# A hybrid encoder block on one core: meta keys of four heads transposed at once, and fillers of the matmul queue placed otherwise

## The chip, the core and the metric

The kernel runs on one core of a Trainium2 chip. A core has a matrix engine (PE, whose weight loads are listed apart as PEld), a vector engine (DVE), an activation engine (ACT), a general engine (POOL) and SP, which here only issues DMAs. Each takes its instructions in the order of its own queue, and engines wait for each other through semaphores. The metric is the device time of one execution in microseconds (us); lower is better.

## What is computed

One encoder layer on 512 tokens, 16 learned meta tokens and width 1024, all in float32. Two token mixers run side by side and are merged by sigmoid gates; an output projection and a gated feed-forward follow.

```python
u = rms_norm(h, pre_mix_gain[l])
proj = u @ w_in[l]
qa, ka, va, qb, kb, vb, g = jnp.split(proj, SPLITS, axis=-1)
...
o_swa = windowed_gqa_sink_attention(qa, ka, va, attn_sink[l], pos, is_real)
...
o_diff = differential_attention(qb, kb, vb, lam, lambda_init, diff_subln_gain[l], is_key)
gates = jax.nn.sigmoid(g + b_gate[l])
g_swa, g_diff = gates[..., :D_MODEL], gates[..., D_MODEL:]
merged = g_swa * (o_swa @ w_branch_swa[l]) + g_diff * (o_diff @ w_branch_diff[l])
h = h + rms_norm(merged @ w_out[l], post_mix_gain[l])
```

In the windowed attention (SWA), 16 query heads share 4 key heads, and a block of 128 queries sees two or three blocks of 128 keys, the 16 meta keys and a sink. The differential attention has 8 heads over all 528 keys, each with two softmaxes.

## The kernel before

Every float32 operand is split into a high part, rounded to a format that PE takes at full rate, and a low part, the rest; a product of two operands is three PE products (high-high, high-low, low-high, `mm3`, lines 286 to 288). A weight tile of 1024 x 128 therefore costs a DMA (`wr`), an ACT cast (`wh`), a subtraction on POOL or DVE (`wl`) and 8 x 3 matmuls into one of three PSUM banks `pr`.

**Start.** Keys and values of SWA are projected by hand-ordered code (to line 479). A transposed row of norms gives `rbc`; DVE multiplies the table `rot` of rotations by it (line 458) and then rotates keys and queries (`ta`, `tb`, line 528) and scales the values (`VT`, line 562), which PE transposes (lines 568 and 573).

**Both attentions** are written as tasks with estimated costs and priorities; `Plan.run` (line 175) places them by list scheduling and so sets each engine's order by hand. Weights of gates and later heads are *fillers*: PE takes three of their matmuls whenever an attention step isn't ready. Which filler may be taken where is written in a few loops (lines 929 to 967).

**SWA** works in 16 units (4 key heads x 4 query blocks). For each of four query heads of a unit PE makes the scores `Sw` (line 674), DVE adds the mask and finds the minimum (line 677), ACT takes the exponential (681), DVE the reciprocal (686), POOL scales `p` (688). Queries reach their place by 16 DMAs `Q<-hl` for each group of four heads (line 550). Then PE transposes `p` block by block, four transposes at a time into one of two banks `tr` (line 705); ACT and DVE split the result into `ah` and `al`, and PE multiplies by the values into the one bank `O` (line 717). The 16 meta keys are a block of their own: four transposes of 128 x 16, an ACT cast and a DVE subtraction of 16 x 512 into rows 0 to 15 and 32 to 47 of `aTm`, and one product with `Vm` (line 710). `O` is emptied through `otmp` and `of`.

**Differential attention** has the same steps (`Sd` line 808, `Od` lines 853 to 863). After the last head, a chain of ACT and DVE steps gives `dh`, `dl`, the split output, eight tiles along the contracted axis. The last branch product (`w_bd`, lines 981 to 987) contracts over these eight for each of eight output tiles, all eight in order for one tile before the next. Then `w_out`, the norms and the feed-forward follow.

## Time and profile before

| quantity | value |
|---|---|
| median of 3 runs | 998.64 us (998.15 to 1000.51) |
| the profiled execution's own time | 999.2 us |
| its span in the profile | 997.3 us |
| mean granted PE clock | 0.992 |

The span runs from the first to the last instruction of the program; 1.9 us of the profiled execution's time lie around it. Busy time of an engine is the time in which some instruction of it was under way. A matmul's record lasts longer than the step to the next one, since matmuls are pipelined; what a matmul costs in a stream is the step between two starts. "Idle before" an instruction, with what ended it, is the time in which its engine had nothing under way.

### The profile page before, as it was taken

The numbers are of one execution on the slowest core, as the hardware profiler recorded it, in microseconds if no ns is written. First come the engines' busy times: TensorE is split into PE (matmuls) and PEld (weight loads), VectorE is DVE, ScalarE is ACT, GpSimd is POOL, SyncE is SP. The second block draws the span as 40 slices with busy tenths as digits, with TensorE's granted clock in tenths as the row PEclk, the third lists the DMA queues.
The fourth block names the chain that finished last, engine by engine and source line by source line (L and its number), as shares of the span: only waits on it lengthen the run. The fifth ranks groups of instructions, "written<-read, shape, count | busy, mean of one in ns | idle before, by whom it ended". The sixth has DMA issues, their size and how long they took to land.

```text
span 997.3 us, 14285 instructions
## 1 busy us (share of the span) xinstructions
PE 969.2 (97%) x5355; PEld 833.7 (84%) x5355; DVE 574.1 (58%) x1015; ACT 451.8 (45%) x828; POOL 278.7 (28%) x242
## 2 busy tenths in 40 slices
PE   9899999999999999999998999999999999999997
PEld 9777887889898999989886888998888888888885
DVE  5746876888575668888774756843332423323224
ACT  6336865785545544577645333633232322312221
POOL 1344344533223332334202412463433400000000
PEclk9999999999999999999999999999999999999999
DMA  9483122141534324415431461353233232234212
GB/s 332 136 213 85 43 78 80 35 129 64 130 100 112 104 68 129 128 46 156 141 106 57 147 219 41 107 170 106 88 103 98 93 105 91 100 103 130 64 64 84
DMA packets 37140, 109.33 MB, mean 110 GB/s; under 512 B 6080, under 2 KB 6592, under 8 KB 37072
## 3 DMA queue, kind: packets, MB, share of 16 engines
q1 hardware_dynamic: 37072, 108.42, 36.1%
q8 instruction: 42, 0.69, 0.3%
q14 instruction: 26, 0.21, 0.1%
HBM read 87.04 MB, written 2.10 MB: 89 GB/s over the span
## 4 chain that ended last, share of the span: by engine, by line
PE 86%; DVE 7%; ACT 3%; issue 2%; SPq 1%; DMA 1%; DVEq 0%; ACTq 0%
PE pr L287 18%; PE pr L288 18%; PE pr L286 18%; PE Sd L808 3%; PE wk L288 2%; PE wk L286 2%; PE Sw L674 2%; PE wk L287 2%; PE tr L705 2%; PE O L717 2%; PE tr L288 2%; PE tr L287 2%; PE tr L286 2%; PE tr L848 2%; PE Od L861 1%
## 5 line engine op out<-in xcount | busy, mean ns | idle before, releaser
L252 POOL TENSOR_TENSOR wl<-wr,wh 128x768 fp32r<-128x768 f32 (+1 forms) x76 | 167.9, 2210 | 242.0 <-ACT wh L271 158.1
L286 PE MATMUL pr<-xh,wh 128*128 128x264 f32 (+1 forms) x616 | 201.2, 327 | 0.0
L288 PE MATMUL pr<-xh,wl 128*128 128x264 f32 (+1 forms) x616 | 197.4, 320 | 0.3 <-DVE wl L252 0.2
L287 PE MATMUL pr<-xl,wh 128*128 128x264 f32 (+1 forms) x616 | 197.4, 320 | 0.2
L271 ACT CAST wh<-wr 128x1024 fp32r<-128x1024 f32 x78 | 82.0, 1052 | 224.6 <-PE pr L287 88.8
L252 DVE TENSOR_TENSOR wl<-wr,wh 128x1024 fp32r<-128x1024 f32 (+2 forms) x110 | 109.8, 999 | 117.6 <-ACT wh L271 108.5
L288 PEld LDWEIGHTS pr<-xh,wl 128*128 128x128 f32 x616 | 116.8, 190 | 9.3 <-POOL wl L252 0.5
L287 PEld LDWEIGHTS pr<-xl,wh 128*128 128x128 f32 x616 | 117.1, 190 | 7.9 <-DVE xl L378 0.6
L286 PEld LDWEIGHTS pr<-xh,wh 128*128 128x128 f32 x616 | 117.1, 190 | 7.3 <-ACT wh L256 0.2
L287 PE MATMUL pr<-ul,wh 128*128 128x512 f32 (+1 forms) x304 | 110.7, 364 | 0.3 <-DVE ul L252 0.3
L286 PE MATMUL pr<-uh,wh 128*128 128x512 f32 (+1 forms) x304 | 110.9, 365 | 0.0
L288 PE MATMUL pr<-uh,wl 128*128 128x512 f32 (+1 forms) x304 | 110.6, 364 | 0.0
L503 ACT CAST wh<-wr 128x1024 fp32r<-128x1024 f32 x56 | 58.4, 1048 | 39.4 <-PE pr L287 31.3
L287 PEld LDWEIGHTS pr<-ul,wh 128*128 128x128 f32 x304 | 57.3, 189 | 9.7 <-DVE ul L252 0.5
L288 PEld LDWEIGHTS pr<-uh,wl 128*128 128x128 f32 x304 | 57.4, 189 | 9.1
L286 PEld LDWEIGHTS pr<-uh,wh 128*128 128x128 f32 x304 | 57.3, 189 | 9.0
L540 POOL TENSOR_TENSOR ta<-ta,tb 128x528 f32<-128x528 f32 (+1 forms) x26 | 36.3, 1395 | 87.9 <-DVE tb L528 77.4
L813 DVE TENSOR_REDUCE nm<-Sd 128x1 f32<-128x528 f32 x64 | 45.1, 704 | 17.5 <-PE Sd L808 16.4
L308 POOL TENSOR_TENSOR r3y<-r3v,mhalf 128x1 f32<-128x1 f32 x4 | 2.2, 549 | 186.7 <-DVE r3v L307 186.7
L688 POOL TENSOR_SCALAR p<-p,rc 128x272 f32<-128x272 f32 (+1 forms) x64 | 37.0, 591 | 61.2 <-DVE rc L686 59.6
L816 ACT ACTIVATE pp<-Sd,nm 128x528 f32<-128x528 f32 x40 | 28.0, 700 | 46.4 <-DVE nm L813 27.7
L808 PE MATMUL Sd<-Kd,Qd 128*128 128x264 f32 x256 | 43.3, 291 | 3.3 <-ACT pp L816 3.1
(366 smaller groups left out, 2003.4 us busy)
## 6 DMA issues: line engine op xcount, KB each, us to landing
wr<-in_w_in_dram SPq DMA_DIRECT2D x50, 512.0 KB, 4.0
wr<-in_w_fi_dram SPq DMA_DIRECT2D x50, 512.0 KB, 3.5
wr<-in_w_fo_dram SPq DMA_DIRECT2D x22, 512.0 KB, 3.4
Kd<-hl SPq DMA_DIRECT2D x32, 132.0 KB, 2.4
Kd<-Kd SPq DMA_DIRECT2D x16, 264.0 KB, 3.4
Q<-hl SPq DMA_DIRECT2D x64, 64.0 KB, 2.0
Qd<-hl SPq DMA_DIRECT2D x64, 64.0 KB, 2.7
wr<-in_w_bs_dram SPq DMA_DIRECT2D x8, 512.0 KB, 3.5
```

The costliest lines, as they stand in the source:

```text
L252: (eng or dve).tensor_tensor(out=lo, in0=src, in1=hi.bitcast(F32), op=ALU.subtract)
L271: act.copy(out=wh, in_=raw)
L286: pe.matmul(out=ps, lhsT=ah, rhs=bh, start=first, stop=False)
L287: pe.matmul(out=ps, lhsT=ah, rhs=bl, start=False, stop=False)
L288: pe.matmul(out=ps, lhsT=al, rhs=bh, start=False, stop=last)
L503: T("ACT", 1.05, lambda: act.copy(out=wh.t, in_=wr.t), r=[wr], w=[wh], prio=pr_)
L540: T("POOL", 0.05 + 1.3 * m, lambda: pool.tensor_tensor(out=ta.t[:, :, 0:n], in0=ta.t[:, :, 0:n], in1=tb.t[:, :, 0:n], op=ALU.add), r=[tb], ...
L674: pe.matmul(out=Sw2[:, S.slot, 0:nk], lhsT=QS[g][hh].t[:, i * P:(i + 1) * P], rhs=KB[g].t[:, x, r0:r1], start=(x == 0), stop=(x == 1))
L688: T("POOL", 0.2 + 0.43 * c, lambda z=z: pool.tensor_scalar(out=pt.t[:, z, 0:nk], in0=pt.t[:, z, 0:nk], scalar1=rc.t[:, z:z + 1], scalar2=1 ...
L808: pe.matmul(out=S.t[:, s, 0:HALF], lhsT=Q[c].t[:, i * P:(i + 1) * P], rhs=K[c].t[:, x, s * HALF:(s + 1) * HALF], start=(x == 0), stop=(x = ...
L813: T("DVE", 0.71, lambda S=S, c=c, one=one: dve.tensor_reduce(out=nm.t[:, c, one], in_=S.t[:, :, 0:HALF], axis=AX.XY, op=ALU.min), r=[S], w ...
L816: T("ACT", 0.9, lambda S=S, c=c, one=one, p=p: act.activation(out=p().rearrange("p (a b) -> p a b", a=2), in_=S.t[:, :, 0:HALF], func=AF.E ...
```

## The change

**Meta keys of SWA.** The 16 meta columns of four heads are first copied by POOL into one tile `pm` of 128 x 128 (each head's 16 twice). One PE transpose replaces four. ACT makes the high part of all 128 rows (`ma`), and four DVE instructions write, for each head, 32 rows of a block-diagonal operand (16 rows high part with its sign turned, 16 rows low part; two columns of signs are new in `vec`). The product with `Vm` is still one matmul, with `Vm` repeated for the four heads and now the last of its unit. Two such operands (`aTm`, `bdm`) take turns. The meta rows of the values are prepared likewise. `otmp` and `of`, through which `O` is emptied, become one tile `ot`.

```diff
+        def meta():
+            tm, w, pm = bank("tr", 2, "tr"), sb("ma", [P, P], F32R, "ma", 3), sb("ma", [P, 4, 2, NMETA], F32, "pm", 3)
...
+            T("POOL", 0.34, lambda: pool.tensor_copy(
+                out=pm.t, in_=pt.t[:, :, mo:mo + NMETA].unsqueeze(2).broadcast_to([P, 4, 2, NMETA])),
+                r=ph, w=[pm], keep=[pt], prio=0)
+            Ttr[u].append(T("PE", 0.14, lambda: pe.transpose(
+                out=tm.t[:, 0:P], in_=pm.t.rearrange("p a b c -> p (a b c)"), identity=ident),
+                r=[pm], w=[tm], prio=0, chain="tr"))
+            T("ACT", 0.32, lambda: act.copy(out=w.t, in_=tm.t[:, 0:P]), r=[tm], w=[w], prio=1, chain="ah")
+            for hh in range(4):
+                rs, cs = slice(32 * hh, 32 * hh + 32), slice(hh * P, (hh + 1) * P)
+                T("DVE", 0.24, lambda rs=rs, cs=cs: dve.scalar_tensor_tensor(
+                    out=bd[rs, cs], in0=tm.t[rs, 0:P], scalar=low[rs], in1=w.t[rs].bitcast(F32), op0=ALU.mult,
+                    op1=ALU.subtract), r=[tm, w], w=[D_], prio=1)
...
+            if n == 0:
+                meta()
...
+        T("PE", mm_t(512), lambda: pe.matmul(out=O.t, lhsT=VM[g // 2].t[:, g % 2].rearrange("p a b -> p (a b)"),
+                                             rhs=bd, start=False, stop=True), r=[D_, VM[g // 2]], w=[O], prio=0)
```

**The table of rotations** becomes a task with a late priority, and the first three weight loads are told to land sooner.

```diff
-    dve.tensor_tensor(out=rot, in0=rot, in1=rbc.unsqueeze(1).broadcast_to([P, 3, EXT]), op=ALU.mult)
...
+    T("DVE", 1.84, lambda: dve.tensor_tensor(out=rot, in0=rot, in1=rbc.unsqueeze(1).broadcast_to([P, 3, EXT]),
+                                             op=ALU.mult), w=[ROT], prio=5)
...
-          w=[wr], dep=dep, prio=pr_, land=3.6)
+          w=[wr], dep=dep, prio=pr_, land=3.6 if nfill[0] > 3 else 0.3)
```

DVE's order at the start, where `rb` are columns of the norms and `kraw` the raw keys; before:

```order
L454 COPY rb<-r0y 128x128
L458 TENSOR_TENSOR rot<-rot,rbc 128x1584
L528 TENSOR_TENSOR ta<-kraw,rot 128x528
L528 TENSOR_TENSOR tb<-kraw,rot 128x528
L528 TENSOR_TENSOR ta<-kraw,rot 128x528
L562 TENSOR_TENSOR VT<-tr,rbc 128x264 x2
```

and the same place in the changed kernel:

```order
L456 COPY rb<-r0y 128x128
L567 TENSOR_TENSOR VT<-tr,rbc 128x264 x2
L630 TENSOR_TENSOR rot<-rot,rbc 128x1584
L471 ISA lj,ls<-lt 128x64
L471 ISA ls 128x1
```

The values `VT` now stand ahead of `rot` and of the three rotations.

**Fillers.** Gates 2 to 5 are released behind units 0, 1, 2 and 8 instead of 2 and 3 behind units 1 and 5; two gates instead of four stay behind SWA; the branch products of SWA are spread 4, 3, 0, 1 instead of 3, 3, 2 over the differential heads.

```diff
-        for j in {1: (2,), 5: (3,)}.get(u, ()):
+        for j in {0: (2,), 1: (3,), 2: (4,), 8: (5,)}.get(u, ()):
...
-    for j in (4, 5, 6, 7):
+    for j in (6, 7):
...
-        for _ in range((3, 3, 2, 0, 0, 0, 0, 0)[h]):
+        for _ in range((4, 3, 0, 1, 0, 0, 0, 0)[h]):
```

SP's order ahead of the first scores, where `Q` are the queries of the first group, `hl` their rotated source and `wr` weights; before:

```order
L501 DMA wr<-in_w_in_dram 128x1024 x3
L550 DMA Q<-hl 32x512 x12
L501 DMA wr<-in_w_in_dram 128x1024 x2
L550 DMA Q<-hl 32x512 x4
L501 DMA wr<-in_w_in_dram 128x1024
```

and in the changed kernel:

```order
L506 DMA wr<-in_w_in_dram 128x1024 x2
L555 DMA Q<-hl 32x512 x8
L506 DMA wr<-in_w_in_dram 128x1024
L555 DMA Q<-hl 32x512 x4
L506 DMA wr<-in_w_in_dram 128x1024
L555 DMA Q<-hl 32x512 x4
L506 DMA wr<-in_w_in_dram 128x1024
```

The last four queries now stand behind one load that directly precedes them instead of two; the other load stands four queries earlier.

**The last branch product** takes the first seven of the eight contracted tiles for output tiles 0 and 1, and only then the eighth for both.

```diff
+    first = [(load_w(I["w_bd"][j]), pr_t()) for j in range(2)]
+    for b in first:
+        bd_products(b, range(KT - 1))
     for j in range(KT):
-        w = load_w(I["w_bd"][j])
-        pb = pr_t()
-        proj(pb, w, (dh, dl), 0, NTOK)
+        b = first[j] if j < 2 else (load_w(I["w_bd"][j]), pr_t())
+        bd_products(b, range(KT - 1 if j < 2 else 0, KT))
+        pb = b[1]
```

PE's order where the eighth tile of `dh` is first needed (the row that waits for ACT), before:

```order
L287 MATMUL pr_5964<-dl_4018,wh_5960 128x512
L288 MATMUL pr_5964<-dh_4017,wl_5961 128x512
L286 MATMUL pr_5964<-dh_4017,wh_5960 128x512 [waits Activation_49]
L287 MATMUL pr_5964<-dl_4018,wh_5960 128x512 [waits DVE_49]
L288 MATMUL pr_5964<-dh_4017,wl_5961 128x512
L286 MATMUL pr_6000<-dh_4017,wh_5995 128x512
```

and in the changed kernel, where `pr_6001` is output tile 0 and `pr_6009` output tile 1:

```order
L287 MATMUL pr_6009<-dl_4309,wh_6004 128x512
L288 MATMUL pr_6009<-dh_4308,wl_6005 128x512 [waits DVE_49]
L286 MATMUL pr_6001<-dh_4308,wh_5997 128x512 [waits Activation_49]
L287 MATMUL pr_6001<-dl_4309,wh_5997 128x512 [waits DVE_49]
L288 MATMUL pr_6001<-dh_4308,wl_5998 128x512
L286 MATMUL pr_6009<-dh_4308,wh_6004 128x512
```

Twenty-one products of output tile 1 now stand between the seventh and the eighth contracted tile of output tile 0.

## Prediction

> **What bounds the kernel now.** I read first the page's busy times and its chain of work, then PE's waits, longest first, then the stages.

> ```profile
> PE 969.2 (97%) x5355; PEld 833.7 (84%) x5355; DVE 574.1 (58%) x1015; ACT 451.8 (45%) x828; POOL 278.7 (28%) x242
> ...
> PE 86%; DVE 7%; ACT 3%; issue 2%; SPq 1%; DMA 1%; DVEq 0%; ACTq 0%
> ```

> PE is busy for 97% of the span and makes 86% of the chain. So a matmul less, or a PE wait less, shortens the run; time saved on another engine does so only where PE waits for it. Where it waits:

> ```profile
> PE Sw L674 <- DVE nm L677: 4.2, 9, 0.9
> PE pr L286 <- ACT dh L898: 4.1, 1, 4.1
> ...
> PE Sw L674 <- issue: 2.1, 1, 2.1
> PE tr L568 <- DVE VT L562: 1.8, 1, 1.8
> ...
> PE tr L573 <- DVE VT L562: 1.1, 1, 1.1
> ```

> Four single waits make 9.1 us: 4.1 for the last head's output, 2.1 ahead of the first scores, 1.8 and 1.1 for the values at the start. The change touches all four. By stage (span, then PE busy, PEld, DVE, ACT, POOL, granted clock):

> ```profile
> 74.90:225.00 150.10, 145.06 (x806) 120.07 (x807) 114.40 (x295) 107.22 (x260) 63.63 (x92) 0.98 0.27 75
> 225.00:536.50 311.50, 306.59 (x2015) 276.41 (x2013) 219.69 (x387) 173.45 (x323) 87.53 (x64) 1.00 0.37 104
> ...
> 545.00:985.00 440.00, 439.66 (x2091) 370.23 (x2091) 181.03 (x236) 134.17 (x185) 98.85 (x55) 1.00 0.33 104
> ```

> SWA (75 to 225) and differential attention (225 to 536) each leave PE idle for about 5 us (150.1 less 145.1; 311.5 less 306.6). From 545 on PE has no slack: what is gained ahead of it reaches the end.

> Idle PE time costs a second time, through the clock:

> ```profile
> 29.24:32.65 3.41, 1.54 (x13) 1.14 (x12) 3.41 (x10) 0.43 (x1) 1.70 (x1) 1.00 0.02 7
> 32.65:36.07 3.42, 3.42 (x18) 3.42 (x17) 3.36 (x8) 3.42 (x8) 2.68 (x2) 0.50 0.01 2
> 73.61:77.03 3.42, 1.68 (x8) 1.23 (x9) 1.07 (x4) 0.71 (x4) 1.81 (x1) 1.00 0.24 47
> 77.03:80.44 3.41, 3.41 (x12) 2.84 (x13) 0.93 (x4) 2.21 (x7) 0.00 (x0) 0.50 0.31 123
> ...
> 537.83:541.24 3.41, 0.51 (x1) 0.19 (x1) 2.73 (x4) 1.34 (x2) 1.19 (x1) 1.00 0.19 38
> 541.24:544.65 3.41, 3.25 (x8) 2.59 (x9) 2.06 (x3) 1.04 (x1) 1.30 (x1) 0.50 0.31 123
> ```

> Each time, a stretch of 3.41 us in which PE was busy for at most 1.7 us is followed by one at a clock of 0.50. In the third a product of 512 columns steps by 0.43 us (below) instead of 0.23; eight of them lose 8 x 0.20 = 1.6 us, which I take for each stretch.

> **A. Meta transposes.** Three of four go, in 16 units.

> ```profile
> 102.14 0.60 PE L705 MATMUL tr<-ident,p 128*128 128x128 f32 x4
> 104.35 0.60 PE L705 MATMUL tr<-ident,p 128*16 128x128 f32 x4
> ...
> 119.55 1.04 PE L705 MATMUL tr<-ident,p 128*128 128x128 f32 x8
> 120.34 0.48 PE L286 MATMUL pr<-xh,wh 128*128 128x512 f32 x1
> 120.66 0.39 PE L287 MATMUL pr<-xl,wh 128*128 128x512 f32 x1
> ```

> Eight transposes and a product take 120.66 - 119.55 = 1.11 us; less 0.23 for the product, 0.11 each. Four of 16 columns last as long as four of 128 (0.60), so 48 transposes are 48 x 0.11 = **5.3 us** of PE, in a stage in which PE is busy for 97%.

> In their place other engines get work:

> ```profile
> L688 POOL TENSOR_SCALAR p<-p,rc 128x400 f32<-128x400 f32 x32 | 20.9, 667 | 28.4 <-DVE rc L686 28.4
> L688 POOL TENSOR_SCALAR p<-p,rc 128x272 f32<-128x272 f32 x32 | 16.1, 516 | 32.8 <-DVE rc L686 31.2 <-PE pr L288 1.6
> L252 DVE TENSOR_TENSOR aTm<-tr,aTm 16x512 fp32r<-16x512 f32 x16 | 10.9, 680 | 3.2 <-ACT aTm L580 2.9
> L580 ACT CAST aTm<-tr 16x512 fp32r<-16x512 f32 x16 | 9.2, 574 | 5.1 <-PE tr L705 4.9
> ...
> L252 DVE TENSOR_TENSOR Vm<-tr,Vm 16x128 fp32r<-16x128 f32 x2 | 0.5, 269 | 0.0
> L580 ACT CAST Vm<-tr 16x128 fp32r<-16x128 f32 x2 | 0.5, 246 | 0.9 <-PE tr L568 0.9
> ```

> POOL: (667 - 516)/128 = 1.18 ns for an element, so the copy of 128 takes 516 - 144 x 1.18 = about 0.35 us; 16 are 5.6 us on an engine busy for 64 of 150. ACT: 0.25 for 0.57, less. DVE: four of 128 elements, 4 x 0.27 = 1.08 for 0.68, so 0.40 more in each unit, 6.4 in all. PE waits for DVE in this stage, so this costs between nothing (all beside PE's products) and 6.4 (all ahead of scores). It is not below nothing, as no DVE work goes. DVE's 114.4 us of work leave PE 4.2 us of waits, which is near the lower end: I take **2 us lost**.

> **B. The last branch product.**

> ```profile
> 526.72 2.09 POOL L252 TENSOR_TENSOR wl<-wr,wh 128x768 fp32r<-128x768 f32 x1 [20.53 <-ACT wh L271]
> ...
> 540.65 0.69 DVE L252 TENSOR_TENSOR dl<-ob,dh 128x512 fp32r<-128x512 f32 x1 [0.68 <-ACT dh L898]
> ...
> 540.67 0.51 PE L286 MATMUL pr<-dh,wh 128*128 128x512 f32 x1 [4.12 <-ACT dh L898]
> 541.40 0.80 PE L287 MATMUL pr<-dl,wh 128*128 128x512 f32 x1 [0.22 <-DVE dl L252]
> 541.99 0.63 PE L288 MATMUL pr<-dh,wl 128*128 128x512 f32 x1
> 542.42 0.63 PE L286 MATMUL pr<-dh,wh 128*128 128x512 f32 x1
> ```

> PE stops at 536.55 (540.67 less 4.12), having done seven of the eight contracted tiles of output tile 0 as it is. The change puts 7 x 3 = 21 products of output tile 1 there: 21 x 0.23 = 4.8 us, against 4.1 + 0.2 of waits. Their low weights are done at 528.8. The chain to `dh` is not touched, so PE comes to it at 541.4, when `dl` is just ready (541.3): 4.3 us of waits go, and the slow clock with them, 1.6: **5.9 us**. The cover has 0.5 us to spare; what the chain is later than that is lost.

> **C. The start.**

> ```profile
> 27.23 1.81 DVE L458 TENSOR_TENSOR rot<-rot,rbc 128x1584 f32<-128x1584 f32 x1 [0.98 <-ACT rbc L457]
> ...
> 30.93 0.77 DVE L562 TENSOR_TENSOR VT<-tr,rbc 128x264 f32<-128x264 f32 x2
> ```

> The values (0.77) now come first, at 27.2, and are ready at 28.0 instead of 31.7. PE asks for them nine products after the transposes of the norms, at about 27.5, so 0.6 remains of 1.8 + 1.1; the second half stands behind 39 products instead of 24. With the wait the clock's drop at 32.65 goes: 2.3 + 1.6 = **3.9 us**. Late instead are `rot` and the key rotations, by 0.8 us; the keys are not needed before the first scores.

> **D. The first scores.**

> ```profile
> 57.97 8.71 SPq L550 DMA_DIRECT2D Q<-hl  x12
> 66.80 2.26 SPq L501 DMA_DIRECT2D wr<-in_w_in_dram  x2
> 69.11 2.41 SPq L550 DMA_DIRECT2D Q<-hl  x4
> ...
> 74.89 0.85 PE L674 MATMUL Sw<-KK,Q 128*128 128x272 f32 x4 [2.11 <-issue]
> ...
> DMA to landing us min/median/max: 1.9/3.1/5.9
> ```

> The page names no releaser, but the last four queries, issued from 69.11 behind two weight loads, land up to 5.9 us later, at 75.0: that is the wait. The queries follow from PE's products, so they come 3.9 us earlier with C, and now behind one load: issued at 65.2, landed between 68.3 (median) and 71.1. PE comes to the scores at 72.8 - 3.9 + 1.4 (six more filler products) = 70.3. I take the wait as gone, as one load less lies ahead, and the drop at 77.03 too: 2.1 + 1.6 = **3.7 us**; from the other end 0.8 of it stays.

> **Fillers.** Gates that move earlier can take at most SWA's 5.0 us of idle time, and can leave open at most one gate's products later, 24 x 0.23 = 5.5. PE's idle share in the later stage is 1.6%, so I stay near nothing: **1 us lost**.

> Sum: 5.3 + 5.9 + 3.9 + 3.7 = 18.8 gained, 3 lost, net 15.8. The profiled execution's 999.2 (span 997.3, and 1.9 around it) becomes 983.4. The median of the runs, 998.64, lies 0.6 lower: **983 us**.

> **Rivals.**

> 1. *The queries stay late.* SP still issues weight loads between them, each of which waits for a subtraction, and these wait for PE. Then D gives nothing: 983 + 3.7 = 986.7. For it: SP was held 2.3 us at 66.80. Against: the products come earlier by C.
> 2. *DVE takes A back.* All 6.4 us fall ahead of scores: 983 + 4.4 = 987.4. For it: the nine waits of `Sw` for DVE. Against: DVE is busy for 76% of the stage.
> 3. *The last product does not cover.* If `dh` is late by as much as the 21 products are long, B gives nothing: 988.9. Against: the chain's order is unchanged.
> 4. *The clock does not follow short gaps.* Then the two drops behind the waits of 1.8 and 2.1 us stay, 2 x 1.6 = 3.2 us: 986.2. Against: these drops begin at 32.65 and 77.03, right after stretches with PE busy for 1.54 and 1.68 us of 3.41. [...]
> 5. *Slower: PE waits out the meta chain.* The block-diagonal product now ends each unit and frees `O`. If PE stood at it for the whole chain of POOL, transpose, ACT and four DVE steps, 0.35 + 0.28 + 0.25 + 1.08 = 2.0 us in 16 units, that is 31 us, less the 2 counted: 1012. It decides from 1.1 us a unit on (17.6 us, more than the net with the 2 counted back). Against: other blocks' products and fillers stand between transpose and product.

> **How the numbers follow.** Chances: forecast 0.54; rivals 0.18, 0.12, 0.06, 0.06, 0.04 in this order. The range goes down to 976, with fillers that take SWA's idle time (983 - 1 - 5 = 977) and a little for sizes; and up to 991, with the first two rivals together (983 + 3.7 + 4.4). That leaves out the slower rival and the edges. A measurement tells about 0.3%, 3 us, from no change: faster is below 995.6, which all cases but the last give, less something for several at once: 0.93; same 0.03; slower 0.04.

> **What will show it.** Right: no PE wait over 1 us for `VT`, ahead of the first `Sw`, or for `dh`; one clock drop or none between 26 and 545; 16 transposes of `pm`, about 0.11 us each; DVE busy some 6 us more in SWA, its waits by PE under 6.2. Wrong: PE waits at the product of `bdm` or `aTm`, or at the transpose of `pm` for POOL; a new wait in the differential stage beyond its 5 us; clock drops without gaps.

## The result, and the profile after

The changed kernel takes 983.19 us (median of 4 runs, 981.71 to 984.33) against 999.58 (998.15 to 1001.96) of the kernel before on the same chip: a ratio of 0.9833, 95% interval 0.9807 to 0.9859. The forecast was 983. The total holds, but only some of its terms do: two were too large, one loss was too small, and a gain stood where a small loss was forecast. Errors of 4 to 5 us cancelled, so that it is luck that the total came this close.

The page of the changed kernel, engines' busy times and the chain:

```profile
PE 960.4 (98%) x5307; PEld 825.3 (84%) x5307; DVE 572.5 (58%) x1061; ACT 446.1 (45%) x828; POOL 287.8 (29%) x262
...
PE 84%; DVE 8%; DMA 3%; issue 2%; SPq 2%; ACT 2%; DVEq 0%; POOL 0%; ACTq 0%
```

PE still sets the time, with 48 instructions fewer (5355 to 5307). Its waits, longest in sum first (who waited for whom: sum, times, longest one, in us):

```profile
PE Sw L692 <- DVE nm L695: 4.5, 13, 1.0
PE tr L585 <- DVE VT L567: 2.8, 3, 1.6
PE Sw L692 <- DMA Q<-hl: 1.9, 1, 1.9
...
PE Sd L840 <- ACT pp L848: 0.7, 1, 0.7
...
PE tr L741 <- DVE bdm L732: 0.6, 1, 0.6
```

The wait of 4.1 for `dh` is gone. The waits for the values (`VT`) and for the queries (`Q`) at the start, which were forecast to go or nearly so, are there. In the differential attention the waits of scores for `pp` are small (0.7 us, against 3.1 before).

By stage, from the first scores to the last product into `O`, from there to the first product on `dh`, and from there on (length, then busy time of PE, PEld, DVE, ACT, POOL, granted clock). Before:

```profile
74.89:224.23 149.34, 144.30 (x800) 119.36 (x801) 113.94 (x295) 106.90 (x258) 62.87 (x91) 0.98 0.27 75
224.23:531.62 307.39, 302.48 (x1999) 273.38 (x1998) 219.60 (x387) 168.88 (x317) 88.30 (x65) 1.00 0.38 106
531.62:985.00 453.38, 448.70 (x2122) 377.06 (x2121) 188.03 (x243) 141.78 (x197) 102.60 (x56) 1.00 0.32 103
```

and after:

```profile
74.42:230.26 155.84, 149.65 (x835) 123.73 (x836) 130.24 (x351) 104.83 (x264) 69.54 (x108) 0.99 0.28 79
230.26:522.98 292.72, 290.20 (x1910) 261.87 (x1909) 204.11 (x380) 165.52 (x313) 86.56 (x62) 1.00 0.38 107
522.98:970.00 447.02, 446.68 (x2121) 375.81 (x2120) 186.77 (x243) 141.72 (x197) 102.60 (x56) 1.00 0.33 104
```

The first scores start at nearly the same time as before (74.4 for 74.9). SWA is 6.5 us *longer* and holds 35 more PE instructions: 75 more projection products and 8 more scores of the next stage, less 48 transposes. The differential stage is 14.7 shorter and PE idles there for 2.5 us instead of 4.9.

To compare stages with unequal content, I count every PE instruction at the step that it has in an undisturbed stream (in the traces of before and after 0.227 us for 512 columns, 0.181 for 400, about 0.12 for 256 to 272, 0.109 for a transpose) and call what is left of the stage the rest; half of the time at a clock of 0.50 is the clock's part of it, an estimate from the step of 512 columns in such a stretch (0.43 us, before, at 542). The 0.227 are 0.44 ns a column, the same as for the bf16 products of 128 columns at the start (0.056 us from 6.4 us on, after); a float32 transpose of 128 columns takes 0.85.

| stage | before: work + rest (clock) | after: work + rest (clock) | rest without clock |
|---|---|---|---|
| start to first scores | 64.6 + 9.3 (1.7) | 65.9 + 7.5 (0) | 7.6 to 7.5 |
| SWA | 133.2 + 16.2 (3.4) | 137.2 + 18.6 (1.7) | 12.8 to 16.9 |
| differential, up to `dh` | 291.5 + 15.9 (0) | 280.8 + 11.9 (0) | 15.9 to 11.9 |
| from the last branch product on | 451.3 + 7.2 (1.7) | 451.3 + 1.0 (0) | 5.5 to 1.0 |

Against the forecast's terms: PE's work 5.4 us less (forecast 5.3), waits ahead of and at the first scores 0.1 less (4.4), SWA 4.1 more (2 more), the differential stage 4.0 less (1 more), the last product 4.5 less (4.3), the clock 5.1 less (4.8).

### The profile page after: what moved, and what is told of

It reads as the page before. It is cut to its first block, busy times and chain, and to the rows that moved or that the text cites. A ratio compares the mean times of both kernels' runs of the same rounds, so it can differ in the third digit from the quotient of the medians.

```text
span 982.5 us, 14257 instructions
## 1 busy us (share of the span) xinstructions
PE 960.4 (98%) x5307; PEld 825.3 (84%) x5307; DVE 572.5 (58%) x1061; ACT 446.1 (45%) x828; POOL 287.8 (29%) x262
## 4 chain that ended last, share of the span: by engine, by line
PE 84%; DVE 8%; DMA 3%; issue 2%; SPq 2%; ACT 2%; DVEq 0%; POOL 0%; ACTq 0%
PE pr L287 18%; PE pr L288 18%; PE pr L286 18%; PE Sd L840 3%; PE Sw L692 2%; PE wk L288 2%; PE wk L286 2%; PE wk L287 2%; PE tr L288 2%; PE tr L287 2%; PE tr L286 2%; PE tr L880 2%; PE O L748 1%; PE Od L893 1%; PE acc L288 1%
## 5 line engine op out<-in xcount | busy, mean ns | idle before, releaser
L252 POOL TENSOR_TENSOR wl<-wr,wh 128x768 fp32r<-128x768 f32 (+1 forms) x76 | 170.8, 2248 | 235.0 <-ACT wh L271 155.7
L286 PE MATMUL pr<-xh,wh 128*128 128x264 f32 (+1 forms) x616 | 200.3, 325 | 0.0
L287 PE MATMUL pr<-xl,wh 128*128 128x264 f32 (+1 forms) x616 | 196.5, 319 | 0.4 <-DVE xl L380 0.4
L288 PE MATMUL pr<-xh,wl 128*128 128x264 f32 (+1 forms) x616 | 196.5, 319 | 0.3 <-POOL wl L252 0.3
L271 ACT CAST wh<-wr 128x1024 fp32r<-128x1024 f32 x78 | 81.9, 1052 | 216.5 <-PE pr L287 84.4
L252 DVE TENSOR_TENSOR wl<-wr,wh 128x1024 fp32r<-128x1024 f32 (+2 forms) x110 | 107.7, 980 | 121.0 <-ACT wh L271 109.1
L288 PEld LDWEIGHTS pr<-xh,wl 128*128 128x128 f32 x616 | 116.0, 188 | 9.0 <-POOL wl L252 0.5
L287 PEld LDWEIGHTS pr<-xl,wh 128*128 128x128 f32 x616 | 116.3, 189 | 8.1 <-DVE xl L380 0.6
L286 PEld LDWEIGHTS pr<-xh,wh 128*128 128x128 f32 x616 | 116.3, 189 | 7.4
L287 PE MATMUL pr<-ul,wh 128*128 128x512 f32 (+1 forms) x304 | 110.7, 364 | 0.3 <-DVE ul L252 0.3
L286 PE MATMUL pr<-uh,wh 128*128 128x512 f32 (+1 forms) x304 | 110.9, 365 | 0.0
L288 PE MATMUL pr<-uh,wl 128*128 128x512 f32 (+1 forms) x304 | 110.6, 364 | 0.0
L508 ACT CAST wh<-wr 128x1024 fp32r<-128x1024 f32 x56 | 58.6, 1049 | 43.7 <-PE pr L287 32.8
L287 PEld LDWEIGHTS pr<-ul,wh 128*128 128x128 f32 x304 | 57.4, 189 | 9.7 <-DVE ul L252 0.5
L288 PEld LDWEIGHTS pr<-uh,wl 128*128 128x128 f32 x304 | 57.3, 189 | 9.1
L286 PEld LDWEIGHTS pr<-uh,wh 128*128 128x128 f32 x304 | 57.3, 189 | 9.0
L845 DVE TENSOR_REDUCE nm<-Sd 128x1 f32<-128x528 f32 x64 | 45.2, 705 | 21.8 <-PE Sd L840 20.9
L699 ACT ACTIVATE p<-p,nm 128x273 f32<-128x273 f32 (+1 forms) x64 | 36.7, 574 | 18.7 <-DVE nm L695 18.3
```

The source lines that it names most:

```text
L252: (eng or dve).tensor_tensor(out=lo, in0=src, in1=hi.bitcast(F32), op=ALU.subtract)
L271: act.copy(out=wh, in_=raw)
L286: pe.matmul(out=ps, lhsT=ah, rhs=bh, start=first, stop=False)
L287: pe.matmul(out=ps, lhsT=ah, rhs=bl, start=False, stop=False)
L288: pe.matmul(out=ps, lhsT=al, rhs=bh, start=False, stop=last)
L508: T("ACT", 1.05, lambda: act.copy(out=wh.t, in_=wr.t), r=[wr], w=[wh], prio=pr_)
```

## Experiments

Each kernel is timed against the kernel before, in turns on one chip (999.3 to 1000.3 us there). "After" means the changed kernel; its 983.19 us are from another session, and each interval reaches about 2 us to either side, so that a difference of some 2 us from after is not resolved.

**1. DVE's four steps twice.**

```diff
-  dve.scalar_tensor_tensor(out=bd[rs, cs], in0=tm.t[rs, 0:P], scalar=low[rs], ...)
+  for _ in range(2):
+      dve.scalar_tensor_tensor(out=bd[rs, cs], in0=tm.t[rs, 0:P], scalar=low[rs], ...)
```

> The changed kernel with each of the four DVE steps that fill the block-diagonal operand done twice (same result written again; planned costs and order as they are). This adds 64 x 0.27 = 17.3 us of DVE work to SWA and nothing else. If the forecast's share is right (2 us lost of 6.4 us added work, 31%), the time rises by 5.4 us, from 983.2 to about 988.6. If DVE's work stands ahead of the scores in full (rival 2), by 17.3, to 1000.5. If it is all beside products, not at all: 983. The comparison of the two traces (about 3.4 us more stall of PE in SWA for 6.4 us of work, 53%) gives 9 us: 992.

Measured: 1002.38 us, ratio 1.0023 (1.0011 to 1.0036); 19.2 us more than after. A step takes 0.35 us in the trace, not the 0.27 of the expectation, so that the 64 more steps add 22.2 us of DVE work, not 17.3 (all 128 steps of this kernel: busy time in us, mean of one in ns | idle before):

```profile
L734 DVE SCALAR_TENSOR_TENSOR bdm<-tr,vec,ma 32x128 fp32r<-32x128 f32 x64 | 22.2, 347 | 2.1 <-ACT ma L729 0.4
L734 DVE SCALAR_TENSOR_TENSOR aTm<-tr,vec,ma 32x128 fp32r<-32x128 f32 x64 | 22.2, 347 | 1.7
```

PE's order is the same as after, and its waits in this kernel are:

```profile
PE Sw L692 <- DVE nm L695: 7.2, 14, 1.7
PE tr L743 <- DVE aTm L734: 5.7, 4, 1.5
PE O L750 <- DVE al L252: 5.4, 7, 1.7
PE tr L743 <- DVE bdm L734: 3.9, 3, 2.1
```

These steps in SWA, where PE's order does not change to meet them, are paid for the most part (19.2 of 22.2 us, 86%), not by a third: they stand in DVE's queue ahead of the split `al`, the next minimum and the next use of a `tr` bank, and PE waits at all of these. DVE is busy for 130 of the 156 us of SWA after, but its place in the chain counts, not its share.

**2. The removed transposes put back.**

```diff
-  pe.transpose(out=tm.t[:, 0:P], in_=pm.t..., identity=ident)
+  for z in range(4):
+      pe.transpose(out=tm.t[:, z * P:(z + 1) * P], in_=pm.t..., identity=ident)
```

> The changed kernel with the transpose of the repeated meta probabilities done four times (three more into unused columns of the same bank), so that PE has as many meta transposes as before the change: 48 more. If these cost PE 0.11 us each on the path, as the forecast has it, the time rises by 5.3 us, from 983.2 to 988.5. If they ride in the time in which PE waits for DVE in this stage (4.5 us of waits for the row minimum), it rises by less than 2 us: 983 to 985.

Measured: 984.67 us, ratio 0.9848 (0.9828 to 0.9867): 1.5 more than after, not 5.3. SWA took 156.6 us instead of 155.8 with 48 PE instructions more. But after has its slow-clock stretch in SWA (1.7 us lost) and this execution has its own ahead of it, at 38.2: without the clock SWA is 2.4 us longer. In SWA, then, PE's order as it stands has time for about half of them: what these take, waits lose.

**3. The last branch product as before.**

```diff
-  first = [(load_w(I["w_bd"][j]), pr_t()) for j in range(2)]
-  for b in first:
-      bd_products(b, range(KT - 1))
   for j in range(KT):
-      b = first[j] if j < 2 else (load_w(I["w_bd"][j]), pr_t())
-      bd_products(b, range(KT - 1 if j < 2 else 0, KT))
+      b = (load_w(I["w_bd"][j]), pr_t())
+      bd_products(b, range(KT))
```

> The changed kernel with the last branch product in the order of before (all eight contracted tiles of one output tile, then the next). If the forecast's step is right, 4.3 us of waits for the last head's output come back and a slow-clock stretch of 3.41 us behind them (1.6 us): 983.2 + 5.9 = 989.1. If the clock does not follow, 987.5 and no stretch at 0.50 after the wait. If the gain came from elsewhere, 983 to 985.

Measured: 988.08 us, ratio 0.9879 (0.9861 to 0.9898): 4.9 more than after. In the trace the wait and the slow clock are back (the row of PE, then the stretches around it with PE's busy time first):

```profile
528.49 0.50 PE L286 MATMUL pr<-dh,wh 128*128 128x512 f32 x1 [4.12 <-ACT dh L930]
```

```profile
525.59:529.00 3.41, 0.50 (x1) 0.19 (x1) 2.73 (x4) 1.34 (x2) 1.25 (x1) 1.00 0.19 30
529.00:532.41 3.41, 3.20 (x8) 2.52 (x9) 2.10 (x4) 1.04 (x1) 1.25 (x1) 0.50 0.31 126
```

From the first product on `dh` to PE's last it takes 458.4 us, as before, against 452.2 after: 6.2 us for this step. The profiled execution as a whole is only 2.7 us longer than that of after, since its first scores began at 72.8 instead of 74.4; why the medians differ by 4.9 and not 6.2 is not shown.

**4. The queries' moves together.** In the plan each of the four moves of a head's queries waits for the landing of the one ahead, because all write one buffer. Here each writes a part of its own, and the scores wait for the four.

```diff
-  move(..., [hl], [QS[g][hh]])
+  T("SP", 0.6, lambda ...: sp.dma_start(...), r=[hl], w=[QB[g][hh][b]], keep=[QS[g][hh]], dep=[slot], prio=2, land=2.7)
...
-  Ssteps[u].append(T("PE", ..., prod, r=[QS[g][hh], KB[g]], w=[S], keep=[S0], prio=1))
+  Ssteps[u].append(T("PE", ..., prod, r=QB[g][hh] + [KB[g]], w=[S], keep=[S0, QS[g][hh]], prio=1, chain="S"))
```

> The changed kernel, with the four moves of a head's queries no longer planned one behind another's landing: the 16 moves of four heads then stand together, ahead of the next weight loads. If the first scores wait for the fourth round of moves, which stand behind a weight load of 512 KB, the wait of 1.9 us ahead of the first scores goes, and with it the slow-clock stretch at 74.6 (1.6 us): 983.2 - 3.5 = 979.7. If another thing comes as late (keys, or the weights of the fillers, now behind 16 moves), PE waits there instead and the time stays within 2 us of 983.2.

Measured: 982.07 us, ratio 0.9823 (0.9804 to 0.9841), not resolved from after. The moves do stand together, in SP's queue of this kernel:

```profile
60.33 11.96 SPq L673 DMA_DIRECT2D Q<-hl  x16
```

and the first scores start at 67.25 instead of 74.42, but PE waits 1.5 us for queries there too: the plan, which now has them earlier, places the scores earlier and takes 36 products of fillers out of the start. The wait moved with them, and so the experiment leaves the price of the wait itself open.

**5. The meta keys as before**, with the fillers' table as changed.

```diff
-  tm, w, pm = bank("tr", 2, "tr"), sb("ma", ...), sb("ma", ...)
...
+  if kb < 0:
+      split_t(lambda: aTm[0:16, :], lambda: aTm[32:48, :], lambda tr=tr: tr.t[0:16, :], [tr], AM, AM, 0.58, chain="ah")
```

> The changed kernel with the meta keys as before: four transposes, the split over 16 rows, the small values' split, and the two tiles of the output's sum apart; all else (fillers, start, last product) as changed. As forecast (5.3 us of transposes less 2 us of DVE work), undoing costs 3.3: 983.2 + 3.3 = 986.5. If DVE's work counts in full, as it did when it was doubled (19.2 us for 64 x 0.27 = 17.3), and the transposes count as little as they did when 48 were added (1.5 us), undoing gains 6.4 - 1.5 = 4.9: 978.3. If only PE counts: 988.5.

Measured: 990.05 us, ratio 0.9907 (0.9891 to 0.9923): 6.9 more. Taken alone this says that the meta part is worth more than its transposes. But SWA became 6.6 us shorter (149.2); what was lost was lost later: PE idles 8.4 us in the differential stage (307.0 less 298.6) instead of 2.5.

**6. One DVE step for four.** The low and high parts of four heads stand below each other, and four products of 128 columns use values with zeros outside the head's rows.

```diff
-  for hh in range(4): T("DVE", 0.24, ... out=bd[rs, cs], in0=tm.t[rs, 0:P], scalar=low[rs] ...)
-  T("PE", mm_t(512), ... lhsT=VM[g // 2]..., rhs=bd ...)
+  T("DVE", 0.24, ... out=bd, in0=tm.t[:, 0:P], scalar=low ...)
+  for hh in range(4): pe.matmul(out=O.t[:, hh * P:(hh + 1) * P], lhsT=M4[g].t[:, hh], rhs=bd, ...)
```

> The changed kernel with the four DVE steps of a unit made one over 128 x 128 (the low and high parts of the four heads stand below each other, not in a block diagonal), and the one product of 512 columns made four of 128, each with values that are zero outside the head's rows (made once for four units by POOL). Takes 48 x 0.26 = 12.5 us of DVE's work out of SWA and adds 48 products of 128 columns, 5.3 us of PE. If DVE counts in full and PE's short work by 1.5 of 5.3, as the two runs before showed: 983.2 - 12.5 + 1.5 = 972. If DVE counts by 31%, as forecast, and PE in full: 983.2 - 3.9 + 5.3 = 984.6.

Measured: 994.63 us, ratio 0.9952 (0.9935 to 0.9968): worse than either theory. Again SWA is shorter, by 6.3 us (149.5), and again PE idles 8.4 us in the differential stage. Its 16 DVE steps of 0.34 us stand for 64 of 0.35, 16.7 us of DVE work less, but as a test of DVE's price the run is inconclusive: the plan was made anew for other costs, with a table made for the old ones.

**7. The fillers' tables as before.**

```diff
-  for j in {0: (2,), 1: (3,), 2: (4,), 8: (5,)}.get(u, ()):
+  for j in {1: (2,), 5: (3,)}.get(u, ()):
...
-  for _ in range((4, 3, 0, 1, 0, 0, 0, 0)[h]):
+  for _ in range((3, 3, 2, 0, 0, 0, 0, 0)[h]):
```

> The changed kernel with the two tables of fillers as before: gates 2 and 3 behind units 1 and 5, gates 4 to 7 behind SWA, branch products 3, 3, 2 by head. As forecast, the fillers' new places cost 1 us: 982.2. If they are what took 4.0 us of PE's idle time out of the differential stage (15.3 to 11.3 us beside its products), 987.2. If they fill waits of SWA, waits of PE there rise above the 6.2 us of the changed kernel.

Measured: 1010.29 us, ratio 1.0103 (1.0081 to 1.0125): 27 us more than after, and slower than before. The stages of this kernel, SWA and the differential one, and its waits:

```profile
75.25:246.10 170.85, 157.67 (x888) 130.78 (x889) 137.84 (x355) 107.75 (x269) 73.77 (x112) 0.99 0.26 72
246.10:548.85 302.75, 289.43 (x1857) 258.54 (x1855) 209.44 (x375) 167.78 (x313) 78.98 (x59) 0.98 0.37 102
```

```profile
PE Sw L692 <- DVE nm L695: 9.4, 16, 2.3
PE Sd L840 <- ACT pp L848: 5.0, 3, 1.8
PE tr L585 <- DVE VT L567: 4.6, 5, 1.6
PE tr L880 <- DVE pp L861: 3.6, 3, 1.7
```

SWA swallows 53 more PE instructions and is 15 us longer; the differential stage has that many fewer and PE idles there for 13.3 us. The profile has five slow-clock stretches against one after (mean granted clock 0.989 against 0.997), which is 6.8 of the 27 us. With the new meta part in place, these few numbers are worth more than any other part of the change.

**8. The values ahead of the key rotations on DVE.**

```diff
-  ... op=ALU.mult), r=[pv[h]], w=[vt], prio=4)
+  ... op=ALU.mult), r=[pv[h]], w=[vt], prio=1)
```

> The changed kernel with the scaling of the values given priority over the key rotations on DVE. PE's two waits for the second pair's values (0.7 and 1.6 us) go: 983.2 - 2.3 = 980.9, and 1.6 less where a slow-clock stretch follows them (979.3). If the keys, which become late by 0.9 us, hold the first scores instead, the time stays within 1 us of 983.2.

Measured: 990.78 us, ratio 0.9915 (0.9898 to 0.9931), 7.6 more, outside both expectations. One wait of 1.7 us for the values stays, and the loss is 400 us later. In the differential stage of this kernel PE waits:

```profile
PE Sd L840 <- ACT pp L848: 2.9, 3, 1.9
PE pr L288 <- DVE wl L252: 2.6, 1, 2.6
PE Sd L840 <- DMA wr<-in_w_in_dram: 1.5, 1, 1.5
```

A priority on DVE at 35 us opened waits at 430, and two slow-clock stretches in a row stand there (mean granted clock of the run 0.994). From here on, undoing a part without a table made for it tests the table.

**9. The meta part alone, on the kernel before**: all of the change to the meta keys, none of those to start, fillers and last product.

```diff
+  if n == 0:
+      meta()
...
-  split_t(lambda: aTm[0:16, :], lambda: aTm[32:48, :], lambda tr=tr: tr.t[0:16, :], [tr], AM, AM, 0.58, chain="ah")
```

> The kernel before with the meta part of the change alone (one transpose for four heads, the block-diagonal operand, the values' signs, the joined output tile); start, fillers and last branch product as before. As forecast, 5.3 us of transposes less 2 us: 1000.1 - 3.3 = 996.8. If the fillers' table decides (with the old table the changed kernel took 1010.3, and the last product and the start are worth about 5 and 2 us): 1010.3 + 7 = 1017, slower than before. If only PE's work counts: 994.8.

Measured: 1005.98 us against 999.27, ratio 1.0071 (1.0051 to 1.0091): the meta part by itself makes the kernel *slower*. Its two stages, and the longest of PE's waits in the second:

```profile
75.03:231.90 156.87, 149.97 (x826) 122.87 (x826) 129.28 (x350) 105.20 (x264) 71.13 (x110) 0.99 0.28 78
231.90:543.05 311.15, 296.87 (x1924) 265.82 (x1924) 216.47 (x380) 170.55 (x318) 82.33 (x61) 0.99 0.35 100
```

```profile
PE Sd L839 <- ACT pp L847: 9.0, 6, 2.3
```

SWA has about the same length as after (156.9 against 155.8), 7.5 us more than before; the differential stage has fewer products and is still 3.8 us longer, since PE idles 14.3 us there. Behind the last head, where they cover nothing but the end of a chain, stand 39 products of fillers instead of 18.

**10. The meta keys as before, with a table made for them.** The table is the best of many by the plan's own estimate of its end.

```diff
-  for j in range(2):
+  for j in (0, 1, 2):
...
-  for j in {0: (2,), 1: (3,), 2: (4,), 8: (5,)}.get(u, ()):
+  for j in {0: (3,), 1: (4,), 8: (5,)}.get(u, ()):
...
-  for _ in range((4, 3, 0, 1, 0, 0, 0, 0)[h]):
+  for _ in range((1, 5, 1, 1, 0, 0, 0, 0)[h]):
```

> The changed kernel with the meta keys as before, as in the run with them undone, but with a table of fillers chosen anew for it (gates 3, 4, 5 behind units 0, 1, 8; branch products 1, 5, 1, 1). If the 6.9 us which undoing cost there were partly those of a table made for other work, this takes less than 990.0: with the forecast's 3.3 us for the meta keys 986.5. If the meta keys by themselves are worth the 5.3 us of their transposes and more, it stays at 988.5 or above.

Measured: 981.44 us, ratio 0.9821 (0.9798 to 0.9844): 8.6 less than with the other table, and not resolved from after. Its two stages:

```profile
72.51:221.30 148.79, 146.19 (x836) 122.36 (x837) 117.46 (x300) 107.54 (x261) 63.27 (x93) 0.99 0.29 79
221.30:520.11 298.81, 294.75 (x1959) 267.14 (x1958) 210.49 (x381) 166.75 (x314) 85.51 (x62) 1.00 0.38 107
```

Here SWA can be compared with after at nearly equal PE work (48 transposes more, 48 products of 264 columns fewer: 136.7 and 137.2 us of work). It is 7.1 us shorter, and its rest without the clock is 10.4 us instead of 16.9. Between them lie 6.5 us, against 11.3 us of DVE work that the change adds there (64 steps, 22.2 us, for 16 subtractions, 10.9). As the two stand, the meta part gives 5.3 us of PE work and takes 6.5 of waits; the plans differ in other places too, so that it is argued and not shown that all 6.5 come from DVE.

**11. `rot` in its old place**, the first weights planned as before, and gate 6 behind unit 13.

```diff
+  dve.tensor_tensor(out=rot, in0=rot, in1=rbc.unsqueeze(1)..., op=ALU.mult)
...
-  T("DVE", 1.84, lambda: dve.tensor_tensor(out=rot, ...), w=[ROT], prio=5)
```

> The changed kernel with the scaling of rot back ahead of the values, and the first weights planned as before; one gate (6) of the table is placed anew, behind unit 13. As forecast (waits of 2.9 us down to 0.6, and a slow-clock stretch of 1.6), undoing costs 3.9: 987.1. By the two traces (waits of 1.8 and 1.1 us became 0, 0.7 and 1.6): 0.6 and the stretch where it falls: 983.8 to 985.4, with a wait for the values of 1.8 us at about 31 us again.

Measured: 985.23 us, ratio 0.9859 (0.9835 to 0.9884): 2.0 more, in the range worked out from the traces, though the intervals overlap. PE's waits for the values are 2.9 us again (1.8 and 1.0), followed by a slow-clock stretch at 33.6.

**12. The queries together, as in run 4, and all places made for it**: the fillers, four priorities, one slack and the release of the last gates and queries, chosen by the plan's own estimate.

```diff
-  for j in {0: (2,), 1: (3,), 2: (4,), 8: (5,)}.get(u, ()):
+  for j in {0: (1,), 1: (2,), 2: (3,), 4: (4,), 8: (5,), 12: (6,), 13: (7,)}.get(u, ()):
...
-  gate2((4, 5), "kk", 4, S6[1:2], S6[5:6])
-  gate2((6, 7), "kk", 4, S6[3:4], S6[5:6])
+  gate2((4, 5), "kk", 4, S6[0:1], S6[2:3])
+  gate2((6, 7), "kk", 4, S6[1:2], S6[3:4])
```

> The kernel with the queries' moves together (982.1), with all fillers, some slacks and the release of the last gates placed anew, so that PE's waits in SWA and in the differential stage shrink. If these waits (16.5 us beside the products in SWA, 11.2 in the differential stage) are a matter of the fillers' places, the time falls by about 3 us, to 979. If they come from chains that no filler covers, or the new places open others, it stays at 982 or rises.

Measured: 978.06 us (977.39 to 978.52), ratio 0.9790 (0.9767 to 0.9813), the fastest of all: 5.1 less than after. What PE still waits for:

```profile
PE Sw L696 <- DVE nm L699: 5.1, 13, 0.8
PE tr L585 <- DVE VT L567: 2.8, 2, 2.1
PE Od L899 <- DVE dal L252: 1.9, 2, 1.4
```

No wait of scores for `pp` is left among the large ones; the rest of the differential stage up to the last scores is 8.2 us against 11.3. In SWA the waits for the minimum stay: no filler covers them.

## Why the forecast held, step by step

**A, meta transposes.** 16 transposes of `pm` do the work (the tile's rows):

```profile
L726 PE MATMUL tr<-ident,pm x16: 270/272/273, 83.7 to 224.3; 128*128 128x128 f32 x16
```

PE's work fell by 5.4 us. The step that failed is "I take 2 us lost" for DVE, and in it first the price. I took 0.27 us for a step, from a subtraction of 16 x 128; the steps of the changed kernel take 0.35 (75 to 232 us: busy time in us, mean of one in ns | idle before):

```profile
L732 DVE SCALAR_TENSOR_TENSOR aTm<-tr,vec,ma 32x128 fp32r<-32x128 f32 x32 | 11.1, 346 | 0.6
L732 DVE SCALAR_TENSOR_TENSOR bdm<-tr,vec,ma 32x128 fp32r<-32x128 f32 x32 | 11.1, 346 | 1.0 <-ACT ma L729 0.4
```

They are 22.2 us, where the 16 subtractions of before were 10.9: 11.3 us more, not 6.4. DVE's busy time in SWA rose by 16.3 us (113.9 to 130.2), not by some 6; the other 5 came with other work that now falls into the stage. The share that PE pays differs with the plan. From before to after it is 4.1 of the 11.3 us, near the third that I took; against the plan of run 10 it is 6.5 of 11.3, and in an unchanged order 19.2 of 22.2 (run 1). So rival 2, DVE takes A back, names the right mechanism, but that its 6.4 us agree with the 6.5 of run 10 is luck: too low a price, times too high a share. The part by itself shows no gain where the fillers are fitted on both sides (run 10), and costs 6.7 us where they are not (run 9).

**B, the last branch product.** Right: 6.2 us in its stage (run 3), forecast 5.9. `dl` is ready just as PE comes to it. DVE's row of the changed kernel, and PE's:

```profile
532.05 0.69 DVE L252 TENSOR_TENSOR dl<-ob,dh 128x512 fp32r<-128x512 f32 x1 [0.69 <-ACT dh L930]
```

```profile
532.80 0.50 PE L287 MATMUL pr<-dl,wh 128*128 128x512 f32 x1
```

Ready at 532.74, used at 532.80: of the half microsecond that the cover was to have to spare, next to nothing is left.

**C, the start.** Half right. DVE's order there, after:

```profile
27.50 0.77 DVE L567 TENSOR_TENSOR VT<-tr,rbc 128x264 f32<-128x264 f32 x2 [0.98 <-ACT rbc L459]
28.19 1.80 DVE L630 TENSOR_TENSOR rot<-rot,rbc 128x1584 f32<-128x1584 f32 x1
29.90 2.42 DVE L471 CUSTOM_DVE_ANT_0 lj<-lt 128x64 f32<-128x64 f32 x1
...
35.32 0.42 DVE L567 TENSOR_TENSOR VT<-pr,rbc 128x264 f32<-128x264 f32 x1
...
37.28 0.43 DVE L567 TENSOR_TENSOR VT<-pr,rbc 128x264 f32<-128x264 f32 x1
```

The wait for the first values (1.8) is gone entirely. But I read both waits as waits for these; the one of 1.1 was for the second half of the second pair, at 38.2. With `rot` and the key rotations now late, PE waits 0.7 and 1.6 for that pair. 2.9 became 2.3, not 0.6. The clock's 1.6 did come, since no slow stretch follows the two waits (last section); but in run 2, with the same order, one stands at 38.2. Run 11 puts the step at 2.0 us, not resolved from nothing, against 3.9.

**D, the first scores.** Failed, as rival 1 has it. SP's queue, after:

```profile
65.81 0.53 SPq L506 DMA_DIRECT2D wr<-in_w_in_dram  x1
66.40 2.41 SPq L555 DMA_DIRECT2D Q<-hl  x4
69.33 0.34 SPq L506 DMA_DIRECT2D wr<-in_w_in_dram  x1
69.71 2.42 SPq L555 DMA_DIRECT2D Q<-hl  x4
```

I took "issued at 65.2 behind one load" for the last four moves; they are issued from 69.71, 0.6 us later than before. The first queries did not come 3.9 us earlier with C either: they are issued from 58.97, 1.0 us later than before. And of the two loads one only moved ahead of four other queries. The order showed that; I read it as one load less ahead of the last queries, where it was the same two. The load issued at 69.33 lands at 73.86 and the four queries behind it at 74.22 to 74.94. The wait is 1.9 instead of 2.1, and the slow stretch stays (at 74.59).

**Fillers.** The step that failed by most: "1 us lost", with bounds of 5 us either way. With the old tables the changed kernel takes 27 us more (run 7). The bounds were taken from idle time in the kernel before, as if the new SWA left its fillers where they were; but a longer SWA takes more of a fixed stock (53 PE instructions more in run 7), and as many are missing later, where PE then idles for 13.3 us. The new table left 2.5 us of idle time in that stage, 2.4 less than before. How much of the whole gain is the table's cannot be given as one number, since it depends on the meta part: with the new keys the old table loses 27 us, with the old keys the new table loses 8.6 against one made for them (runs 5 and 10). The table alone on the kernel before was not run.

**Rivals 3 and 4** fell: the product covers, the drop at 32.65 went with the wait of 1.8 us ahead of it, and the one at the first scores stayed with a wait of 1.9 (74.59). **Rival 5's** mechanism (PE at the product of the operand) did not come: PE waits 0.6 us for `bdm`, at a transpose. But a slower outcome was near by another way, that of runs 7 and 9: a longer SWA that uses up the fillers. I had not named it. (In rival 5 the bound of 1.1 us a unit is a little low: 17.6 us are not yet more than 15.8 + 2.)

## What to carry to other kernels

Where a list scheduler spreads a fixed stock of fillers, an edit changes the time through the plan that it causes as much as through its own cost: compare variants only with fillers fitted to each, and judge a part by its stage at equal work. An engine that is not the bottleneck can have little slack if its steps stand ahead of something that the bottleneck waits for (here DVE, busy for 130 of the 156 us of SWA: 19.2 of the 22.2 us added in run 1 were paid); doubling the suspected step in an unchanged order shows this in one run, once the step's own time is read from the trace.

## What was not expected of the hardware

```profile
158.95:162.36 3.41, 1.92 (x12) 1.50 (x11) 2.39 (x10) 2.06 (x7) 0.96 (x2) 1.00 0.03 5
162.36:165.77 3.41, 3.41 (x15) 2.97 (x16) 2.63 (x6) 2.08 (x5) 2.31 (x4) 0.50 0.35 101
```

How much of a wait falls into one stretch decides how long PE is busy in it. In the changed kernel the boundary at 37.05 us divides the second wait for the values (1.65 us, until 37.77), and no slow stretch follows; the wait for the queries (1.87 us, until 74.42) lies in one stretch, and a slow one follows:

```profile
33.63:37.05 3.42, 1.83 (x8) 1.04 (x7) 3.39 (x7) 0.47 (x1) 1.70 (x1) 1.00 0.34 138
37.05:40.46 3.41, 2.69 (x14) 2.13 (x15) 3.41 (x4) 2.19 (x5) 3.01 (x3) 1.00 0.00 0
71.18:74.59 3.41, 1.54 (x7) 0.96 (x7) 0.01 (x1) 0.80 (x2) 2.37 (x1) 1.00 0.65 204
74.59:78.01 3.42, 3.42 (x12) 2.80 (x12) 1.09 (x5) 1.12 (x4) 0.00 (x0) 0.50 0.45 153
```

In run 2, with the same order up to there, it is the other way round at the values:

```profile
34.82:38.24 3.42, 1.14 (x6) 0.91 (x7) 3.38 (x7) 1.93 (x4) 2.52 (x2) 1.00 0.01 4
38.24:41.65 3.41, 3.41 (x10) 2.57 (x9) 3.38 (x5) 0.72 (x2) 3.41 (x3) 0.50 0.14 14
```

What sets where the stretches begin is not shown. The forecast's three stretches were right in number by luck: of those at 32.65, 77.03 and 541.24 the second has its counterpart after (74.59), and one that the forecast did not count, at 162.36, is gone.

**A DVE step beside POOL's subtraction took 2.42 us, where it took 0.65 before.** The step is `lj`. Before, it runs beside POOL's `ta` (30.48 to 32.18); the second `lj` of before, with no POOL instruction beside it, took 0.21. After, it runs beside a subtraction of POOL (`wl` of 128x1024) that takes 4.00 us where the median of its shape is 2.40. POOL's subtraction starts at 28.24, while DVE works on `rot` until 29.99, and ends at 32.24; `lj` starts at 29.90 and ends at 32.32. Why both were longer there no run shows. In DVE's queue `lj` stands ahead of the second pair of values, and so is part of what delays it.
